# Scan scores as 64 by 64 blocks in the two column halves of TensorE

## The chip, the cores and the metric

The kernel runs on one core of a Trainium2 chip. The metric is the device time of one execution in microseconds (us).

## The reference

Two layers of a network on 1152 tokens (1024 of a latent sample and 128 of a prompt) with 1024 channels. Layer 0 mixes tokens by Fourier transforms, layer 1 by a gated linear recurrence in both directions (HGRN2, 8 heads with 128 key and 128 value channels); each is followed by an MLP of 4096 channels. What the change touches is the recurrence of layer 1. Cut to what matters:

```python
f = lbh + (1.0 - lbh) * jax.nn.sigmoid(z)      # z: forward and backward gate projections
k = 1.0 - f
...
def step(s, inp):                              # one chunk of tokens
    bcum = jnp.cumsum(gc, axis=-2)             # gc = log f
    o_inter = jnp.einsum('dbhtk,dbhkv->dbhtv', qc * jnp.exp(bcum), s)
    decay = jnp.exp(jnp.where(tril[:, :, None], diff, -jnp.inf))
    scores = jnp.einsum('dbhtk,dbhsk,dbhtsk->dbhts', qc, kc, decay)
    o_intra = jnp.einsum('dbhts,dbhsv->dbhtv', scores, vc)
    s_new = jnp.exp(blast[..., 0, :])[..., None] * s + jnp.einsum('dbhsk,dbhsv->dbhkv', ...)
    return s_new, o_inter + o_intra
```

The score of query t and key s is a product over the key channels with the gates between s and t. The size of a chunk is free in exact arithmetic; the kernel takes chunks of 128 tokens.

## The kernel before

Activations lie channel-major: channels on the 128 partitions, 1152 token columns, in three column chunks of 384 for the projections and MLPs and in nine chunks of 128 (`NK`) for the scan. Weights and activations of the large products are split into a high and a low part, and `mm3` (L85) makes each product from three one-pass matmuls, recorded as L91. The scan's own products are plain float32, which TensorE runs as two weight loads and two matmuls each.

`hgrn` (L634) works head by head. `heads_in(h)` computes the two gate projections and the query of a head (three projections of 72 matmuls), `gates(h)` the output gate (72 more), `values(p)` the values of two heads. `levels(F, q)` (L716) makes the scores of all nine chunks, `finish` (L772) the states, the outputs and their norm. In the loop at L845 head h runs `levels` and `finish`, and the projections of head h + 1 are written after them.

In `levels`, `QK` holds queries and keys with the gates multiplied in, for both directions. Scores are built by doubling block sizes B = 1, 2, ... 64 (seven levels). A first call of `scores` (L740) takes the products of queries and summed keys on the diagonal and has ScalarE copy them from PSUM to `sT` (L741). Each level then has four steps:

- ScalarE copies the keys of the level to `V` (L751; one buffer, so the copy waits for the scores of the level before);
- `scores` (L733) multiplies, for each chunk, 128 keys by 128 queries on TensorE (L737), three chunks to a PSUM buffer; queries of the two directions are read in alternating blocks by `view` (L726), at level 0 column by column;
- VectorE copies each group of three chunks to `sT` where the level's mask says so (`copy_predicated`, L753). The mask of a level selects pairs of tokens in the same block of 2B but different halves of it;
- VectorE multiplies keys and queries by the gates of the level (L762) and halves the list of gates (L765).

```python
def scores(lhs, rhs, done):
    for g in range(NK // 3):
        ps = self.t(pp, [P, 4, P], F32, "o", 3)[:, 0:3, :]
        for i in range(3):
            nc.tensor.matmul(out=ps[:, i, :], lhsT=lhs(3 * g + i), rhs=rhs(3 * g + i), start=True, stop=True)
        done(slice(3 * g, 3 * g + 3), ps)
```

`finish` transposes the keys (L779, copied by ScalarE at L781), updates the states (L786, L799, L825) and sums each chunk's output from scores and states (L818 to L821).

The order of the instructions on each engine is not written out by hand. The framework lists them when the kernel is built, by data dependence, by the order in the program and by its estimate of each instruction's time, so that work of the next head stands between the score calls of one head. At run time every engine takes its list in that order. PSUM has three banks with tag "o" (scores, outputs), three with "z" (projections) and two with "m". The small weight matmuls of `ada_pe` (L156: two weight columns, 512 moving columns, and L165: two rows) belong to layer 0 and are named only because the prediction reads them.

Of the kernel before, what the change touches and what calls it, by code (L numbers as in the profile page):

```python
# [19 lines left out]
P = 128  # L20
# [19 lines left out]
def spans(c):  # L40
    """Column ranges of chunk c with the index of their conditioning vector."""
    a, b = c * CH, (c + 1) * CH
    out = []
    if a < LS:
        out.append((a, min(b, LS), 0))
    if b > LS:
        out.append((max(a, LS), b, 1))
    return out
# [7 lines left out]
class Net:  # L56
# [13 lines left out]
    def tmp(self, *shape):  # L70
        """short-lived float32 rows"""
# [4 lines left out]
    def split(self, pool, src, shape, tag, bufs=None):  # L76
        """src == hi + lo, both in the tensor engine's one-pass float32 format."""
# [7 lines left out]
    def mm3(self, out, pairs, first=True, last=True):  # L85
        """out = sum of lhsT^T rhs over pairs of split operands."""
# [30 lines left out]
    def cond_rows(self):  # L117
        """silu of both conditioning vectors on every partition"""
# [17 lines left out]
    def make_A(self, layer, part, g):  # L136
        """norm weight times (1 + scale)"""
# [6 lines left out]
    def bank(self, tag):  # L144
        """one PSUM bank"""
        return self.t(self.ps, [P, 512], F32, tag, {"z": 3, "o": 3, "m": 2}[tag])

    def ada_pe(self, layer, part, tag):
        """one part of silu(cond) @ ada_w on the tensor engine, then channels onto partitions"""
# [20 lines left out]
    def ada_dve(self, layer, part, rawp, junkp, bufs):  # L170
        """the same on the vector engine: rows of the transposed weight times silu(cond), summed along the row"""
# [15 lines left out]
    def fnet(self):  # L187
# [11 lines left out]
        # tokens: position table, rms, and the sums and differences of the two halves  # L199
# [27 lines left out]
        # with a, b, c, d the tokens l, l + 512, 512 - l and 1024 - l (tokens 256 and 768 stand in c and d at l = 0),  # L227
        # even positions take a + b and c + d, cosines of odd ones (a - b) - (c - d) and sines (a - b) + (c - d)
# [61 lines left out]
        # output map, to be folded over the symmetric channel frequencies  # L290
# [104 lines left out]
        def shift():  # L395
            """what the shift adds to position 0: two more columns, one per conditioning vector"""
# [26 lines left out]
        # the residual, channel-major  # L423
# [74 lines left out]
    def square(self, d, chunks):  # L498
        """add the squares of channel tile d to the running sum"""
# [10 lines left out]
    def rstd(self, chunks):  # L510
        """1/rms of the columns of the chunks, columns on partitions"""
# [14 lines left out]
    def rms(self, chunks, tag):  # L526
        """1/rms of the columns of each chunk, on every partition (in PSUM)"""
# [13 lines left out]
    def norm_h(self, c, rb, A, sh):  # L541
        """modulated norm of chunk c, split, channel-major"""
# [15 lines left out]
    def unit(self, src, pool=None, bufs=2):  # L558
        """one split weight unit"""
# [11 lines left out]
    def mlp(self, layer, before_chunk, before_block, after_chunk):  # L571
# [3 lines left out]
        for blk in range(NBLK):  # L575
# [10 lines left out]
            # the first two units go chunk by chunk, as the norm delivers them  # L586
# [47 lines left out]
    def hgrn(self, xd, after_chunk):  # L634
# [52 lines left out]
        def values(p):  # L687
            """values of two heads, tokens on partitions; each goes where its head's output will replace it"""
# [27 lines left out]
        def levels(F, q):  # L716
# [9 lines left out]
            def view(base, B, c=None):  # L726
                np_, off = (T // (2 * B), 0) if c is None else (P // (2 * B), c * P)
# [5 lines left out]
            def scores(lhs, rhs, done):  # L733
                for g in range(NK // 3):
                    ps = self.t(pp, [P, 4, P], F32, "o", 3)[:, 0:3, :]
                    for i in range(3):
                        nc.tensor.matmul(out=ps[:, i, :], lhsT=lhs(3 * g + i), rhs=rhs(3 * g + i), start=True, stop=True)  # L737
                    done(slice(3 * g, 3 * g + 3), ps)

            scores(lambda c: ks[:, 0, c * P:(c + 1) * P], lambda c: q[:, c * P:(c + 1) * P],  # L740
                   lambda sl, ps: nc.scalar.copy(out=sT[:, sl, :], in_=ps))  # L741
# [387 lines left out]
```

## Time and profile before

| | |
|---|---|
| median of 3 runs | 2748.15 us (2743.88 to 2750.95) |
| span of the profiled execution | 2739.4 us (no other time of that execution is given) |
| TensorE busy, matmuls | 2702.2 us, 99% of the span |
| TensorE busy, weight loads | 2582.3 us, 94% |
| VectorE busy | 1453.2 us, 53% |
| ScalarE busy | 854.4 us, 31% |
| GpSimd busy | 35.8 us, 1% |
| the scan with its projections | from about 1121 to 1850 us of the span |

PE stands for TensorE's matmuls, PEld for its weight loads, DVE for VectorE, ACT for ScalarE, POOL for GpSimd. A busy share of 99% on PE means that some matmul was under way; matmuls overlap, so a sum of their records is more than the time they take, and the pace is read from a run of equal ones. The span is the time from the first to the last instruction; what lies around it is the difference to the run's time.

### The profile page before, as it was taken

Reading aid. Unit: us, or ns where it says so; the run is one execution under the profiler, and the core shown is the slowest. Engines: PE = TensorE matmul, PEld = TensorE weight load, DVE = VectorE, ACT = ScalarE, POOL = GpSimd, SP = SyncE. Lnnn points to the kernel's source line nnn. Section 1 sums busy time; section 2 is a strip of 40 time slices with the busy share of each in tenths; the row PEclk is TensorE's granted clock in tenths of the full one; section 3 lists DMA queues with packets and bytes.
Section 4 is the critical chain, followed back from the end, with each engine's and each line's share of the span. In section 5 each row is a group of like instructions: output and inputs, shape, how many; then the busy total and the mean of one; then the engine's idle time right before and its main releaser. Section 6 shows DMA issues by size and latency. Waiting matters only on the chain.

```text
span 2739.4 us, 39068 instructions
## 1 busy us (share of the span) xinstructions
PE 2702.2 (99%) x16142; PEld 2582.3 (94%) x16142; DVE 1453.2 (53%) x2585; ACT 854.4 (31%) x1678; POOL 35.8 (1%) x44
## 2 busy tenths in 40 slices
PE   8999999999999999999999999999999999999999
PEld 3678999999999999999999999999999999999998
DVE  7778998332332447565673774786433233233335
ACT  5435232133123233322332332343422321321332
POOL 0000000000000000000000000000000000000000
PEclk9999999999999999999999999999999999999999
DMA  7531554111111102101000101031111111111111
GB/s 272 200 130 64 184 192 150 43 47 39 40 48 38 62 24 94 35 25 36 28 29 30 36 28 39 28 104 54 43 38 48 43 39 47 43 36 46 45 33 70
DMA packets 65627, 179.93 MB, mean 66 GB/s; under 512 B 8197, under 2 KB 14725, under 8 KB 65449
## 3 DMA queue, kind: packets, MB, share of 16 engines
q1 hardware_dynamic: 65448, 177.43, 19.5%
q8 instruction: 127, 2.08, 0.3%
q14 instruction: 52, 0.42, 0.1%
HBM read 166.92 MB, written 10.49 MB: 65 GB/s over the span
## 4 chain that ended last, share of the span: by engine, by line
PE 91%; DVE 5%; DMA 2%; issue 1%; ACT 1%; POOL 1%; SPq 0%; DVEq 0%; POOLq 0%; ACTq 0%
PE z L91 45%; PE o L91 29%; PE o L737 5%; PE z L702 4%; DMA adaw<-in_ada 2%; DVE junk L179 1%; PE o L156 1%; PE m L786 1%; PE m L779 1%; DVE QK L762 1%; PE m L156 1%; PE o L821 0%; PE o L818 0%; PE o L820 0%; DVE hl L553 0%
## 5 line engine op out<-in xcount | busy, mean ns | idle before, releaser
L91 PE MATMUL z<-hh,wh 128*128 128x384 f32 x2496 | 841.6, 338 | 2.3 <-ACT wh L81 1.3
L91 PE MATMUL z<-hl,wh 128*128 128x384 f32 x2496 | 837.7, 336 | 0.1
L91 PE MATMUL z<-hh,wl 128*128 128x384 f32 x2496 | 836.5, 336 | 0.0
L91 PEld LDWEIGHTS z<-hh,wh 128*128 128x128 f32 x2496 | 468.5, 188 | 7.1 <-ACT hh L552 2.8
L91 PEld LDWEIGHTS z<-hl,wh 128*128 128x128 f32 x2496 | 469.1, 188 | 2.6 <-DVE hl L553 1.5
L91 PEld LDWEIGHTS z<-hh,wl 128*128 128x128 f32 x2496 | 468.6, 188 | 0.6 <-DVE wl L82 0.5
L567 DVE SCALAR_TENSOR_TENSOR x<-o,mod,x 128x384 f32<-128x384 f32 (+2 forms) x512 | 253.2, 515 | 352.0 <-PE o L91 351.6
L82 DVE TENSOR_TENSOR wl<-raw,wh 128x1024 fp32r<-128x1024 f32 x113 | 138.1, 1223 | 293.0 <-ACT wh L81 292.9
L91 PE MATMUL o<-a1h,w 128*128 128x384 f32 x1024 | 280.6, 335 | 0.3 <-DVE x L567 0.3
L91 PE MATMUL o<-a2h,w 128*128 128x384 f32 x1024 | 279.1, 335 | 0.0
L91 PE MATMUL o<-a0h,w 128*128 128x384 f32 x1024 | 279.0, 335 | 0.0
L605 ACT CAST w<-raw 128x512 fp32r<-128x512 f32 x128 | 79.4, 621 | 611.1 <-PE o L91 596.1
L81 ACT CAST wh<-raw 128x1024 fp32r<-128x1024 f32 x113 | 118.5, 1050 | 258.8 <-PE z L91 230.6
L91 PEld LDWEIGHTS o<-a1h,w 128*128 128x128 f32 x1024 | 186.6, 188 | 1.4 <-DVE x L567 0.9
L91 PEld LDWEIGHTS o<-a2h,w 128*128 128x128 f32 x1024 | 186.6, 188 | 0.8 <-issue 0.5
L91 PEld LDWEIGHTS o<-a0h,w 128*128 128x128 f32 x1024 | 186.6, 188 | 0.5 <-ACT a0h L81 0.2
L582 ACT ACTIVATE s<-z 128x384 f32<-128x384 f32 x192 | 93.6, 489 | 284.1 <-PE z L91 277.7
L91 PE MATMUL o<-a2l,w 128*128 128x384 f32 x512 | 171.9, 336 | 0.4 <-DVE a2l L82 0.4
L91 PE MATMUL o<-a0l,w 128*128 128x384 f32 x512 | 171.4, 335 | 0.1
L91 PE MATMUL o<-a1l,w 128*128 128x384 f32 x512 | 171.2, 334 | 0.1
L762 DVE TENSOR_TENSOR QK<-QK,F 128x1152 f32<-128x1152 f32 x112 | 164.2, 1506 | 0.0
L179 DVE SCALAR_TENSOR_TENSOR junk<-adaw,s_rows 128x1024 bf16<-128x1024 f32 x128 | 156.0, 1219 | 11.7 <-DMA adaw<-in_ada 10.6
(256 smaller groups left out, 3281.6 us busy)
## 6 DMA issues: line engine op xcount, KB each, us to landing
adaw<-in_ada SPq DMA_DIRECT2D x96, 512.0 KB, 3.6
raw<-in_w SPq DMA_DIRECT2D x64, 512.0 KB, 3.3
raw<-in_w SPq DMA_DIRECT2D x128, 256.0 KB, 2.6
raw<-in_win SPq DMA_DIRECT2D x32, 512.0 KB, 3.2
x<-in_xT SPq DMA_DIRECT2D x8, 576.0 KB, 4.4
xd<-x SPq DMA_DIRECT2D x8, 576.0 KB, 2.8
raw<-in_who SPq DMA_DIRECT2D x9, 512.0 KB, 3.9
x<-xd SPq DMA_DIRECT2D x8, 576.0 KB, 4.8
```

The source lines that it names most:

```text
L81: nc.scalar.copy(out=hi, in_=src)
L82: nc.vector.tensor_sub(out=lo, in0=src, in1=hi.bitcast(F32))
L91: self.nc.tensor.matmul(out=out, lhsT=w[a], rhs=h[b], start=first and i == 0, stop=last and i == n - 1)
L156: nc.tensor.matmul(out=rows[i][0:2, :], lhsT=self.s[:, k, :], rhs=w[:, i * 512:(i + 1) * 512], start=k == 0, stop=k == KT - 1)
L179: nc.vector.scalar_tensor_tensor(out=jk, in0=w, scalar=1.0, in1=self.sb[:, b, :], op0=ALU.mult, op1=ALU.mult, accum_out=m[:, j, b:b + 1])
L567: self.nc.vector.scalar_tensor_tensor(out=xs, in0=ps[:, a - c * CH:b - c * CH], scalar=gt[:, d, q:q + 1], in1=xs, op0=ALU.mult, op1=ALU.add)
L582: nc.scalar.activation(out=s, in_=z, func=AF.Relu)
L605: nc.scalar.copy(out=w[:, 0], in_=raw)
L702: nc.tensor.matmul(out=half, lhsT=hs[c][a][:, KT // 2 * hf + k, o:o + P], rhs=ws[hf][b][:, k, :], start=hf == 0 and k == 0 and m == 0, sto ...
L737: nc.tensor.matmul(out=ps[:, i, :], lhsT=lhs(3 * g + i), rhs=rhs(3 * g + i), start=True, stop=True)
L762: nc.vector.tensor_tensor(out=kv, in0=kv, in1=fv, op=ALU.mult)
L779: nc.tensor.transpose(out=pt[:, i * P:(i + 1) * P], in_=QK[:, 2 + dr, c * P:(c + 1) * P], identity=self.ident)
```

## The change

The scores of a chunk are computed as blocks of 64 keys by 64 queries instead of 128 by 128. Block h of a chunk (h = 0, 1) is a matmul with 64 weight columns whose output goes to partitions 64h to 64h + 63, the half of the array's columns that belongs to them. The first call and the levels B = 1 to 32 take only the two blocks on the diagonal, the last level (B = 64) only the two off it (`cross`). A call has two PSUM buffers, of five and four chunks, instead of three of three chunks, and four copies of 64 partitions instead of three of 128. At the last level all of a block is wanted, so it is copied by ScalarE without a mask. The rest of the diff takes out comments. The core of it:

```diff
-            def view(base, B, c=None):
-                np_, off = (T // (2 * B), 0) if c is None else (P // (2 * B), c * P)
+            H2 = P // 2
+
+            def view(base, B, c=None, h=0):
+                np_, off = (T // (2 * B), 0) if c is None else (H2 // (2 * B), c * P + h * H2)
...
-            def scores(lhs, rhs, done):
-                for g in range(NK // 3):
-                    ps = self.t(pp, [P, 4, P], F32, "o", 3)[:, 0:3, :]
-                    for i in range(3):
-                        nc.tensor.matmul(out=ps[:, i, :], lhsT=lhs(3 * g + i), rhs=rhs(3 * g + i), start=True, stop=True)
-                    done(slice(3 * g, 3 * g + 3), ps)
-
-            scores(lambda c: ks[:, 0, c * P:(c + 1) * P], lambda c: q[:, c * P:(c + 1) * P],
-                   lambda sl, ps: nc.scalar.copy(out=sT[:, sl, :], in_=ps))
+            def scores(lhs, rhs, done, cross=0):
+                for cs in ((0, 5), (5, 9)):
+                    n = cs[1] - cs[0]
+                    ps = self.t(pp, [P, 512], F32, "o", 3)[:, 0:n * H2].rearrange("p (n t) -> p n t", t=H2)
+                    for i in range(n):
+                        for h in range(2):
+                            nc.tensor.matmul(out=ps[h * H2:(h + 1) * H2, i, :], lhsT=lhs(cs[0] + i, h),
+                                             rhs=rhs(cs[0] + i, h ^ cross), start=True, stop=True)
+                    for h in range(2):
+                        k = h ^ cross
+                        done(sT[h * H2:(h + 1) * H2, cs[0]:cs[1], k * H2:(k + 1) * H2], ps[h * H2:(h + 1) * H2], n, h, k)
+
+            def half(x, c, h):
+                return x[:, c * P + h * H2:c * P + (h + 1) * H2]
+
+            scores(lambda c, h: half(ks[:, 0], c, h), lambda c, h: half(q, c, h),
+                   lambda out, ps, n, h, k: nc.scalar.copy(out=out, in_=ps))
...
-                m = mask[:, lev, :].unsqueeze(1).broadcast_to([P, 3, P])
+                def merge(out, ps, n, h, k):
+                    if 2 * B == P:
+                        nc.scalar.copy(out=out, in_=ps)
+                    else:
+                        m = mask[h * H2:(h + 1) * H2, lev, k * H2:(k + 1) * H2]
+                        nc.vector.copy_predicated(out=out, mask=m.unsqueeze(1).broadcast_to([H2, n, H2]), data=ps)
...
-                scores(lambda c: V[:, c * P:(c + 1) * P], lambda c: view(0, B, c),
-                       lambda sl, ps: nc.vector.copy_predicated(out=sT[:, sl, :], mask=m, data=ps))
+                if 2 * B == P:
+                    scores(lambda c, h: half(V, c, h), lambda c, h: half(QK[:, h], c, h), merge, 1)
+                else:
+                    scores(lambda c, h: half(V, c, h), lambda c, h: view(0, B, c, h), merge)
```

## Rows read from the trace of the kernel before

**Rows 1.** The page: busy time of TensorE, and the chain that ended last

```profile
PE 2702.2 (99%) x16142; PEld 2582.3 (94%) x16142; DVE 1453.2 (53%) x2585; ACT 854.4 (31%) x1678; POOL 35.8 (1%) x44
...
PE 91%; DVE 5%; DMA 2%; issue 1%; ACT 1%; POOL 1%; SPq 0%; DVEq 0%; POOLq 0%; ACTq 0%
PE z L91 45%; PE o L91 29%; PE o L737 5%; PE z L702 4%; DMA adaw<-in_ada 2%; DVE junk L179 1%; PE o L156 1%; PE m L786 1%; PE m L779 1%; DVE QK L762 1%; PE m L156 1%; PE o L821 0%; PE o L818 0%; PE o L820 0%; DVE hl L553 0%
```

**Rows 2.** Busy us (instructions) in the scan's stretch: PE, PEld, DVE, ACT, POOL; then clock, DMA

```profile
1121.00:1850.00 729.00, 716.29 (x4869) 691.38 (x4868) 476.92 (x700) 227.82 (x524) 20.38 (x24) 1.00 0.11 38
```

**Rows 3.** The chain that ended last, levels of the first head: start, us, what

```profile
1136.56 2.09 PE z L91 x12
1138.65 2.18 PE o L737 x18
1140.82 2.11 PE z L91 x12
```

**Rows 4.** Timeline of VectorE, one level of the first head: start, us

```profile
1139.62 1.84 DVE L753 COPY_PREDICATED sT<-mask,o 128x384 f32<-128x384 uint8 x3
1141.36 2.61 DVE L762 TENSOR_TENSOR QK<-QK,F 128x1152 f32<-128x1152 f32 x2
```

**Rows 5.** Timeline, end of a projection and the first two score calls

```profile
1119.11 0.33 PE L91 MATMUL z<-hl,wh 128*128 128x384 f32 x1
1119.11 0.19 PEld L91 LDWEIGHTS z<-hh,wl 128*128 128x128 f32 x1
...
1121.53 2.17 PE L737 MATMUL o<-q,kT 128*128 128x128 f32 x18
1121.56 1.05 ACT L81 CAST wh<-raw 128x1024 fp32r<-128x1024 f32 x1 [3.50 <-PE z L91]
...
1123.54 3.12 PE L737 MATMUL o<-QK,nacc 128*128 128x128 f32 x18
```

**Rows 6.** Who waited for whom, scan: us in total, times, longest

```profile
PEld o L737 <- issue: 18.7, 46, 1.4
```

**Rows 7.** Timeline, two-column matmuls (L156) between full ones of layer 0

```profile
155.96 0.28 PE L91 MATMUL o<-EY1l,vh 128*128 128x256 f32 x1
...
156.08 0.28 PE L91 MATMUL o<-EY1h,vl 128*128 128x256 f32 x1
...
156.28 0.09 PEld L156 LDWEIGHTS m<-adaw,s_silu 128*2 128x2 f32 x2
156.29 3.59 PE L156 MATMUL m<-adaw,s_silu 128*2 128x512 f32 x8
...
159.81 0.19 PEld L91 LDWEIGHTS z<-EY0h,uh 128*128 128x128 f32 x1 [0.86 <-issue]
159.81 0.39 PE L91 MATMUL z<-EY0h,uh 128*128 128x256 f32 x1
```

**Rows 8.** Groups by line in the scan: busy us, mean ns, idle before

```profile
L753 DVE COPY_PREDICATED sT<-mask,o 128x384 f32<-128x384 uint8 x168 | 99.6, 594 | 15.7 <-PE o L737 10.3
...
L781 ACT COPY kT<-m 128x384 f32<-128x384 f32 x48 | 22.2, 480 | 15.9 <-PE m L779 14.0
...
L799 DVE SCALAR_TENSOR_TENSOR Sb<-Sb,F,m 128x128 f32<-128x128 f32 x56 | 19.4, 346 | 12.3 <-PE m L786 7.2
...
L737 PE MATMUL o<-q,kT 128*128 128x128 f32 x144 | 18.0, 275 | 0.0
...
L683 DVE SCALAR_TENSOR_TENSOR gs<-sg,gn,z 128x384 f32<-128x384 f32 x22 | 13.5, 612 | 19.1 <-ACT sg L652 19.1
...
L741 ACT COPY sT<-o 128x384 f32<-128x384 f32 x24 | 10.9, 484 | 2.6 <-PE o L737 2.6
...
L793 ACT COPY Sf<-m 128x128 f32<-128x128 f32 x16 | 3.9, 266 | 4.6 <-PE m L786 4.6
```

**Rows 9.** Other matmuls (L91) between two score calls, last head: stretch, us, PE busy

```profile
1795.40:1797.80 2.40, 2.40 (x15) 2.26 (x13) 1.00 0.00 0
```

**Rows 10.** Timeline of TensorE, two-row matmuls (L165) of layer 0

```profile
47.03 1.05 PE L165 MATMUL o<-ident,traw 2*128 2x2 f32 x8
```

## The prediction

> **What bounds the kernel now.** I read the page's sums first: TensorE is busy for 2702 of 2739 us and holds 91% of the chain that ended last, the scan's score matmuls (L737) 5% of it [rows 1]. The table by stretch shows that this holds in the scan too (1121 to 1850 us): TensorE 716 of 729 us, VectorE 477, ScalarE 228, at a granted clock of 1.00, the higher of its two levels (2.4 GHz) [rows 2]. So in the scan a microsecond of TensorE is a microsecond of time, as long as TensorE finds other work while a level of the scan waits for VectorE.
>
> The chain inside one head's levels [rows 3] shows how that works: 18 score matmuls, 2.18 us, then 12 matmuls of the next head's projections (L91), 2.1 us, in turn, with no gap. VectorE is just as full there: three masked copies (1.84 us) and two products (2.61 us) follow each other without idle time, so that a level takes 4.27 us by VectorE as well [rows 4]. The two engines are in balance in the levels; outside them VectorE has slack and TensorE has none.
>
> **The change, part by part.** *What the scores cost today.* Each 128x128 float32 product is two weight loads and two matmuls, so nine chunks are 18 pairs. In the first call they take (2.17 - 0.275) / 17 = 0.112 us a pair, 2.01 us in all; at level 0, whose queries are read with a large stride, (3.12 - 0.275) / 17 = 0.167, 3.0 us [rows 5] (one record is 0.275 us [rows 8]). Seven calls at 2.01 and one at 3.0 are 17.1 us a head, 137 us for 8 heads, which is the 5% of the chain.
>
> *What they cost after.* A call has 36 pairs, each with half the weight columns and half the moving columns. No row shows two matmuls in different column halves. If the halves work side by side, a chunk needs half the time; with 2 ns more for twice the instructions, 18 x 0.058 = 1.04 us, at level 0 18 x 0.085 = 1.5 us, 8.8 us a head, 70 us in all: 67 us less. If they don't, a pair of half size costs at least half of 0.112 and the gain is 0. If even size doesn't matter, 36 x 0.112 = 4.0 us a call, 128 us more. I take the first: a pair's load starts with the matmul before it and is shorter with fewer columns (0.09 us with 2, 0.19 with 128) [rows 5, 7], so nothing in a half-wide pair needs the other half of the array. The other two ends are rivals below.
>
> The Trainium skill ("TensorEngine Tiling (Array Packing)", Tiling Modes, Key Properties) says that different tiles can load weights and multiply in parallel, and that a change of tiling mode drains the engine. No run here shows the first; by it the sum stands as it is.
>
> *Going in and out of half-wide mode.* The nearest rows are the two-column matmuls of L156 between full ones [rows 7]. Going in: full matmuls start every 0.12 us, the last at 156.08, the narrow one not at 156.20 but at 156.29: 0.09 us. Coming out: eight narrow ones at 0.428 us end their stream at 159.71; the next full one starts at 159.81 and its record is 0.39 instead of 0.28 us, because its weights were no longer loaded under earlier work: 0.21 us. With half-wide weights exposed on the way in (0.05), that is 0.35 us. Today's entry already loses some of it: before the scores TensorE's loads stood still for 18.7 us in 46 cases [rows 6]. I take 0.3 us. The first call and level 0 stand together, so there are 7 visits a head, 56 in all: 17 us. Bounds 0 and 0.5 us: 0 to 28.
>
> *VectorE.* Three masked copies of 128x384 (0.59 us each) become four of 64 partitions with 320, 320, 256 and 256 columns. A column costs (612 - 346) / 256 = 1.04 ns (L683 against L799) [rows 8], so 0.52 and 0.46 us: 1.96 for 1.77 us, 0.19 more at each of six levels, and 1.77 less at the last. A level's pace by VectorE goes from 4.27 to 4.46 us. That is hidden if TensorE has other work: its scores would leave 4.46 - 1.04 - 0.3 = 3.1 us, 18 projection matmuls of 0.173 us instead of 12. A head's projections have 4 x 72 = 288 and the levels use 72, the second projection's weights are split at 1121.56 us, before the levels begin [rows 5], and three PSUM banks with three gate buffers hold six column chunks, 144 matmuls; 6 x 18 = 108 fit. The order on TensorE is fixed when the kernel is built, by an estimate. That it follows the gap shows in the last head, where 15 matmuls stand in a gap instead of 12 [rows 9]. For gaps not exactly filled I add 3 us. If the cover is missing, rival 2 gives the price.
>
> *ScalarE.* The first call's copies become four, and the last level's four come here from VectorE. At (484 - 266) / 256 = 0.85 ns a column (L741 against L793) [rows 8] they take 0.43 and 0.38 us, 1.6 us together: 0.15 more at the start of a head and 1.6 more at its end. ScalarE is busy for 228 of 729 us, but behind the last level's scores it also copies the transposed keys (L781, 0.48 us each [rows 8]), which free the PSUM banks of TensorE's transposes (L779). If these copies are queued first, up to 1.6 us a head come into TensorE's path, 13 us; projections can stand there, and VectorE drops its 1.77 us at the same place. I take 2 us. A score call now takes two PSUM buffers instead of three, DMA issues don't change, and SP and POOL see nothing: no cost.
>
> *The sum.* -67 + 17 + 3 + 2 = -45 us. The page gives no time of the profiled execution other than its span, 2739.4 us; the median of the runs is 8.75 us above it, which I leave as it is. Span 2694, time 2703. Own range of this case: 2683 (no cost of the mode) to 2725 (0.5 us a visit, ScalarE's copies half on the path).
>
> **The rivals.** *1. The halves don't work side by side (slower).* Its place is the weight load. Eight pairs with two moving columns took 1.05 us [rows 10], 0.13 us each with the last one's tail, against 2.17 / 18 = 0.12 for pairs with 128 [rows 5]: the load sets the pace as much as the stream does. If the loads of the two halves follow each other, a half-wide pair can't go below about 0.056 to 0.060 us, a call takes 2.0 to 2.16 us and the mode comes on top: 17 + 64 x (0 to 0.15) + 2 = 19 to 29 us. Time 2771. It decides from 47 ns a pair on, (2.01 - 0.3) / 36: above that the change loses. For it: in the whole trace loads and matmuls alternate, each load starting with the matmul before it [rows 5, 7]; an order this strict would leave the other half waiting. Against it: that is one array with one set of weights in waiting. Chance 0.32.
>
> *1b.* A half-wide load isn't hidden under a matmul at all: a pair then costs its load and its stream, 0.056 + 0.056 = 0.112 us, 128 + 17 us more, 2893. Every row of the full array shows the load hidden. Chance 0.04. The Trainium skill ("TensorE: Matmul & The Clock Gate", Part 3, "What overlaps and what doesn't") has a rule to this effect: a weight load overlaps a running matmul only where the row group differs, and both halves here use all 128 rows. The trace of the full array disagrees.
>
> *2. The order stays as it is.* The scores get shorter, but twelve matmuls still stand in each gap, and TensorE waits for VectorE's 4.46 us. Then five gaps lose 0.19 each, 0.95 us a head; the first call with level 0 still wins 5.0 - 2.55 - 0.3 = 2.1 and the last level 0.7. Together 1.9 us a head, 15 us: 2733. Chance 0.12.
>
> *3. Part of the overlap.* At 45 to 50 ns a pair gain and mode cost cancel: 2740 to 2756, no change. Chance 0.09.
>
> **How the numbers follow.** The forecast has 0.43. Faster by over 0.3% (8 us, about what a measurement of this kernel can tell from no change): the forecast and rival 2, 0.55. Slower: rivals 1 and 1b, 0.36. Within: rival 3, 0.09. The signs are nearly even, because the one number that decides, the pace of half-wide pairs in turn, is in no row. The range therefore reaches from the forecast's best end to the far end of rival 1, 2683 to 2778; outside it lie 1b and what I have not thought of.
>
> **What would show it.** Right: the 36 score matmuls of a call in about 1.05 us with starts some 29 ns apart on average, gaps with about 18 projection matmuls, L737 at 2 to 3% of the chain, the scan near 685 us. Mode cost: 0.1 us of standstill before the first score and a longer first projection behind the last. Rival 1: starts 56 ns apart or more and the scan longer than 729 us. 1b: 112 ns. Rival 2: TensorE idle for VectorE (L762) in every gap, a level at 4.46 us. The forecast's sign is wrong if the starts are over 47 ns apart.

## The result and the profile after

The changed kernel takes 2717.13 us (median of 4 runs, 2716.04 to 2719.05), the kernel before 2747.97 us in the same series (2743.88 to 2750.95): ratio 0.9894, 95% interval 0.9880 to 0.9908, or 30.8 us less, where 45 us less was forecast. The kernel is faster, by the mechanism of the forecast, and a third of the expected gain is missing.

The page of the changed kernel, its sums and its chain that ended last:

```profile
PE 2659.8 (98%) x17294; PEld 2528.4 (93%) x17294; DVE 1457.8 (54%) x2609; ACT 865.6 (32%) x1718; POOL 35.7 (1%) x44
...
PE 84%; DVE 10%; DMA 3%; issue 2%; ACT 1%; POOL 1%; SPq 0%; DVEq 0%; POOLq 0%; ACTq 0%
PE z L91 42%; PE o L91 30%; PE z L702 4%; DVE QK L783 4%; DVE sT L764 3%; DMA adaw<-in_ada 2%; PE o L156 1%; PE m L807 1%; PE o L744 1%; DVE junk L179 1%; PE m L800 1%; PE o L839 1%; PE m L156 1%; DVE wl L82 0%; PE o L842 0%
```

Against [rows 1] the scores (now L744) fall from 5% to 1% of the chain. VectorE rises from 5% to 10%, with the products (L783) and the masked copies (L764) of the levels: work that was beside TensorE's now stands on the path.

The groups by line, the changed operations (busy us, mean ns of one, then idle time ahead and its releaser):

```profile
L744 PE MATMUL o<-QK,nacc 128*64 128x64 f32 x2016 | 78.6, 233 | 24.6 <-DVE QK L783 23.7
...
L764 DVE COPY_PREDICATED sT<-mask,o 64x320 f32<-64x320 uint8 x96 | 50.1, 522 | 3.4 <-PE o L744 0.7
...
L764 DVE COPY_PREDICATED sT<-mask,o 64x256 f32<-64x256 uint8 x96 | 43.0, 447 | 3.1
...
L744 PE MATMUL o<-q,kT 128*64 128x64 f32 x288 | 11.4, 226 | 0.0
```

The same group of the kernel before (its first calls stand in [rows 8]):

```profile
L737 PE MATMUL o<-QK,nacc 128*128 128x128 f32 x1008 | 133.9, 288 | 8.5 <-DVE QK L762 8.4
```

Twice as many score matmuls are busy for 90 us instead of some 152, but TensorE waits 23.7 us ahead of them for VectorE's products, where it waited 8.4. One level of VectorE in the second head, from its timeline (start, us):

```profile
1212.40 2.03 DVE L764 COPY_PREDICATED sT<-mask,o 64x320 f32<-64x320 uint8 x4
1214.46 2.63 DVE L783 TENSOR_TENSOR QK<-QK,F 128x1152 f32<-128x1152 f32 x2
1217.12 2.04 DVE L764 COPY_PREDICATED sT<-mask,o 64x320 f32<-64x320 uint8 x4
```

From copy to copy it is 4.72 us: 2.06 for the copies and 2.66 for the products. In [rows 4] it was 4.27, with the products 1.74 us behind the copies.

Where the time went shows in two stretches: from the first score of the first head to the first score of the last one, and from there to the next norm. The table by stretch of the kernel before (busy time of each engine, granted clock, DMA share, GB/s):

```profile
1125.00:1784.00 659.00, 648.74 (x4406) 627.45 (x4405) 419.51 (x608) 198.73 (x457) 17.83 (x21) 1.00 0.09 31
1784.00:1873.00 89.00, 86.55 (x570) 82.93 (x568) 68.50 (x109) 33.87 (x73) 2.55 (x3) 1.00 0.32 110
```

and of the changed kernel:

```profile
1125.00:1751.00 626.00, 611.14 (x5446) 578.33 (x5444) 424.20 (x632) 210.41 (x497) 17.83 (x21) 1.00 0.10 33
1751.00:1847.00 96.00, 82.45 (x707) 78.51 (x706) 69.75 (x111) 35.68 (x78) 2.55 (x3) 0.91 0.30 102
```

By the starts of the first score calls, seven heads take 625.4 us instead of 662.7 (37.3 less), but the last head up to the next norm takes 96.3 instead of 88.5 (7.7 more); TensorE is idle there for 13.5 of 96 us, at a granted clock of 0.91, where it was idle for 2.5 of 89 at 1.00. Together 29.6 us less, against 30.8 by the medians. All that follows takes 866.6 us in both. What stands ahead of the scan has the same code and ends between 1121.5 and 1129.8 us in the profiles of this study; its 4.3 us more in this profile are that spread.

The levels themselves did not get shorter. From the start of a head's first score call to the start of its last one it is 29.8 to 30.3 us in seven heads of the kernel before and 30.5 to 31.2 in the changed one: VectorE sets their pace. What got shorter is what stands behind them, since 102 to 106 matmuls of the next head's projections lie in a head's gaps instead of 72. At the 0.173 us from one to the next, 30 to 34 matmuls are 5.2 to 5.9 us (an estimate); each of the seven heads gains 5.1 to 5.5 us.

The last head's scores in TensorE's timeline of the changed kernel (start, us, count, idle time ahead):

```profile
1758.86 1.30 PE L744 MATMUL o<-QK,nacc 128*64 128x64 f32 x36 [0.82 <-DVE QK L783]
...
1763.51 1.27 PE L744 MATMUL o<-QK,nacc 128*64 128x64 f32 x36 [0.16 <-DVE QK L783]
...
1765.52 0.34 PE L91 MATMUL z<-hh,wh 128*128 128x384 f32 x1
1768.22 1.27 PE L744 MATMUL o<-QK,nacc 128*64 128x64 f32 x36 [2.37 <-DVE QK L783]
1772.91 2.19 PE L744 MATMUL o<-QK,nacc 128*64 128x64 f32 x36 [3.42 <-DVE QK L783]
1777.82 2.19 PE L744 MATMUL o<-QK,nacc 128*64 128x64 f32 x36 [2.72 <-DVE QK L783]
1782.73 2.19 PE L744 MATMUL o<-QK,nacc 128*64 128x64 f32 x36 [2.73 <-DVE QK L783]
```

Eighteen filling matmuls (L91) stand ahead of the first of these calls, seventeen ahead of the second, five ahead of the third, and from 1765.9 us on none: four calls alone in 17 us. In [rows 9] and the calls around it there were 15, 15, 15, 12, 12 and 11. From 1771 to 1785 us the table by stretch has a granted clock of 0.50, the lower level (1.2 GHz); ahead of that TensorE stood idle for 2.37 and for 3.42 us with a single call between:

```profile
1771.00:1785.00 14.00, 6.64 (x109) 6.24 (x110) 13.21 (x17) 3.34 (x7) 0.00 (x0) 0.50 0.00 1
```

A call then takes 2.19 us instead of 1.27, but it follows the one before it after 4.91 us instead of 4.71: with VectorE setting the pace, the lower clock costs about 0.2 us in each of three levels there, a small part of what the last head loses.

### The profile page after: what moved, and what is told of

It is laid out like the page before. It is cut to its first block, busy times and chain, and to the rows that moved or that the text cites. A ratio compares the mean times of both kernels' runs of the same rounds, so it can differ in the third digit from the quotient of the medians.

```text
span 2714.1 us, 41391 instructions
## 1 busy us (share of the span) xinstructions
PE 2659.8 (98%) x17294; PEld 2528.4 (93%) x17294; DVE 1457.8 (54%) x2609; ACT 865.6 (32%) x1718; POOL 35.7 (1%) x44
## 4 chain that ended last, share of the span: by engine, by line
PE 84%; DVE 10%; DMA 3%; issue 2%; ACT 1%; POOL 1%; SPq 0%; DVEq 0%; POOLq 0%; ACTq 0%
PE z L91 42%; PE o L91 30%; PE z L702 4%; DVE QK L783 4%; DVE sT L764 3%; DMA adaw<-in_ada 2%; PE o L156 1%; PE m L807 1%; PE o L744 1%; DVE junk L179 1%; PE m L800 1%; PE o L839 1%; PE m L156 1%; DVE wl L82 0%; PE o L842 0%
## 5 line engine op out<-in xcount | busy, mean ns | idle before, releaser
L91 PE MATMUL z<-hh,wh 128*128 128x384 f32 x2496 | 840.0, 338 | 1.6 <-ACT wh L81 0.6
L91 PE MATMUL z<-hl,wh 128*128 128x384 f32 x2496 | 840.7, 337 | 0.1
L91 PE MATMUL z<-hh,wl 128*128 128x384 f32 x2496 | 837.1, 336 | 0.0
L91 PEld LDWEIGHTS z<-hh,wh 128*128 128x128 f32 x2496 | 468.3, 188 | 7.3 <-ACT hh L552 2.7
L91 PEld LDWEIGHTS z<-hl,wh 128*128 128x128 f32 x2496 | 469.0, 188 | 4.5 <-DVE hl L553 1.4
L91 PEld LDWEIGHTS z<-hh,wl 128*128 128x128 f32 x2496 | 468.8, 188 | 0.9 <-DVE wl L82 0.2
L567 DVE SCALAR_TENSOR_TENSOR x<-o,mod,x 128x384 f32<-128x384 f32 (+2 forms) x512 | 253.2, 515 | 352.1 <-PE o L91 351.7
L91 PE MATMUL o<-a1h,w 128*128 128x384 f32 x1024 | 280.7, 335 | 0.0
L91 PE MATMUL o<-a2h,w 128*128 128x384 f32 x1024 | 279.2, 335 | 0.0
L91 PE MATMUL o<-a0h,w 128*128 128x384 f32 x1024 | 279.1, 335 | 0.0
L82 DVE TENSOR_TENSOR wl<-raw,wh 128x1024 fp32r<-128x1024 f32 x113 | 138.3, 1224 | 261.9 <-ACT wh L81 261.1
L91 PEld LDWEIGHTS o<-a1h,w 128*128 128x128 f32 x1024 | 186.7, 188 | 0.8 <-DVE x L567 0.3
L91 PEld LDWEIGHTS o<-a2h,w 128*128 128x128 f32 x1024 | 186.6, 188 | 0.8 <-PE o L91 0.3
L91 PEld LDWEIGHTS o<-a0h,w 128*128 128x128 f32 x1024 | 186.6, 188 | 0.4 <-ACT a0h L81 0.2
L91 PE MATMUL o<-a2l,w 128*128 128x384 f32 x512 | 172.0, 336 | 2.9 <-DVE a2l L82 2.9
L91 PE MATMUL o<-a0l,w 128*128 128x384 f32 x512 | 171.4, 335 | 0.1
L91 PE MATMUL o<-a1l,w 128*128 128x384 f32 x512 | 171.4, 335 | 0.2 <-DVE a1l L82 0.2
L783 DVE TENSOR_TENSOR QK<-QK,F 128x1152 f32<-128x1152 f32 x112 | 165.0, 1513 | 1.5
L179 DVE SCALAR_TENSOR_TENSOR junk<-adaw,s_rows 128x1024 bf16<-128x1024 f32 x128 | 156.1, 1220 | 12.9 <-DMA adaw<-in_ada 11.7
```

The source lines that it names most:

```text
L82: nc.vector.tensor_sub(out=lo, in0=src, in1=hi.bitcast(F32))
L91: self.nc.tensor.matmul(out=out, lhsT=w[a], rhs=h[b], start=first and i == 0, stop=last and i == n - 1)
L179: nc.vector.scalar_tensor_tensor(out=jk, in0=w, scalar=1.0, in1=self.sb[:, b, :], op0=ALU.mult, op1=ALU.mult, accum_out=m[:, j, b:b + 1])
L567: self.nc.vector.scalar_tensor_tensor(out=xs, in0=ps[:, a - c * CH:b - c * CH], scalar=gt[:, d, q:q + 1], in1=xs, op0=ALU.mult, op1=ALU.add)
L783: nc.vector.tensor_tensor(out=kv, in0=kv, in1=fv, op=ALU.mult)
```

## The experiments

All start from the changed kernel. Each series has runs of the kernel before on its own chip, so the ratios are what compares. "Seven heads" and "last head" are the two stretches above, read from each kernel's profile, in us.

| kernel | time, us | before, us | ratio, 95% interval | seven heads | last head |
|---|---|---|---|---|---|
| before | 2747.97 | | 1 | 662.7 | 88.5 |
| changed | 2717.13 | 2747.97 | 0.9894 (0.9880 to 0.9908) | 625.4 | 96.3 |
| e1_halves_in_turn | 2735.56 | 2742.86 | 0.9975 (0.9965 to 0.9984) | 643.3 | 98.3 |
| e2_last_level_masked | 2712.26 | 2742.86 | 0.9889 (0.9876 to 0.9903) | 623.1 | 96.3 |
| e3_copies_over_128 | 2694.31 | 2742.86 | 0.9818 (0.9805 to 0.9832) | 613.7 | 89.4 |
| e4_last_head_filled | 2710.19 | 2742.86 | 0.9883 (0.9870 to 0.9897) | 625.1 | 91.6 |
| after_again | 2712.75 | 2744.62 | 0.9884 (0.9867 to 0.9900) | 625.2 | 97.0 |
| e5_last_head_on_vector | 2716.09 | 2744.62 | 0.9897 (0.9882 to 0.9912) | 625.1 | 95.6 |
| e6_level5_by_scalar_filled | 2715.24 | 2744.62 | 0.9896 (0.9881 to 0.9911) | 630.2 | 92.4 |
| e7_level5_by_scalar | 2717.87 | 2744.62 | 0.9905 (0.9891 to 0.9920) | 630.2 | 94.0 |
| after_third | 2714.59 | 2745.09 | 0.9892 (0.9877 to 0.9907) | 625.2 | 95.5 |
| e8_masked_and_filled | 2710.18 | 2745.09 | 0.9872 (0.9857 to 0.9887) | 623.5 | 93.0 |
| e9_filled_with_less_gpsimd | 2712.47 | 2745.09 | 0.9879 (0.9863 to 0.9896) | 623.2 | 93.3 |

The changed kernel's seven heads repeat within 0.2 us and its last head within 1.5 us. Many of the effects below are smaller than the intervals of the whole time; they are told by these stretches, each read from one execution. The times expected below start from the first series, where the kernel before takes 2747.97 us; in the later ones it takes 3 to 5 us less.

**Do the two halves work side by side?**

```diff
-                    for i in range(n):
-                        for h in range(2):
+                    for h in range(2):
+                        for i in range(n):
```

> All 4 or 5 blocks of the upper half of the columns are computed before those of the lower half, so that neighbouring score matmuls go to the same half; nothing else is changed. Theory (the gain comes from two halves that work side by side): with the neighbours in one half a block takes the 56 to 60 ns that half a pair took before the change, a call takes 2.0 to 2.2 us instead of 1.05 us, and 64 calls give back 1.0 us each less what falls into TensorE's waits for VectorE (some 8 to 12 us): 2765 to 2785 us. Rival (a block of half the size is cheap by itself, whichever half its neighbour is in): starts stay 30 ns apart and the time stays at 2713 to 2721 us.

One call in TensorE's timeline, first of the changed kernel, then of this one:

```profile
1142.56 1.27 PE L744 MATMUL o<-QK,nacc 128*64 128x64 f32 x36 [0.30 <-DVE QK L783]
1143.76 0.44 PE L91 MATMUL z<-hh,wh 128*128 128x384 f32 x1
1144.04 0.34 PE L91 MATMUL z<-hl,wh 128*128 128x384 f32 x1
```

```profile
1219.13 1.77 PE L744 MATMUL o<-QK,nacc 128*64 128x64 f32 x36
```

In the changed kernel's levels the single records start some 22 and 36 ns apart in turn, 58 ns for a block in each half; from the first start to the last a call takes 1.047 us. With the halves in turn, neighbours in one half start 53 to 60 ns apart, a call takes 1.553 us, and the two stretches take 20 us longer (by the ratios the time rises by 0.8 to 0.9% of before, 22 to 25 us). So the halves do work side by side, and a block of half the size isn't cheap by itself: the rival falls. The size was missed, +0.5 us a call where +1.0 was expected. Where a group of blocks in one half gives way to the other half's, records start within 3 to 6 ns of each other: the other half's first blocks start beside the last ones of the half before, nine of 36 in most calls. Order by halves costs half of the overlap, not all of it.

**What is the unmasked copy worth by itself?**

```diff
-                    if 2 * B == P:
-                        nc.scalar.copy(out=out, in_=ps)
-                    else:
+                    if True:
```

> The last level is copied with the mask by VectorE again; the blocks of 64 by 64 stay. The four copies put about 2.1 us back on VectorE once in each head and take four copies from ScalarE. Theory (VectorE's levels are what the order waits for in the changed kernel): up to 2.1 us in each of 8 heads come back, 2725 to 2734 us. Rival (the last level lies beside filling matmuls and ScalarE's copies cost the same wait): 2713 to 2721 us, and the unmasked copy is worth nothing by itself.

The rival holds, and more: seven heads take 2.3 us less with the mask. ScalarE's timeline behind the last level of one head shows why, first of the changed kernel:

```profile
1339.80 1.62 ACT L761 COPY sT<-o 64x320 f32<-64x320 f32 x4 [3.01 <-PE o L744]
1341.44 0.86 ACT L802 COPY kT<-m 128x384 f32<-128x384 f32 x2
```

and of this kernel, where the second line is the first:

```profile
1336.38 0.86 ACT L800 COPY kT<-m 128x384 f32<-128x384 f32 x2 [3.96 <-PE m L798]
```

The four unmasked copies hold ScalarE for 1.62 us ahead of the copies of the transposed keys, which free the banks of TensorE's transposes; on VectorE they cost this stretch nothing. The part "without a mask" costs 0.3 us a head, and the blocks carry the whole gain.

**What do copies of 64 partitions cost?**

```diff
-                    for h in range(2):
-                        k = h ^ cross
-                        done(sT[h * H2:(h + 1) * H2, cs[0]:cs[1], k * H2:(k + 1) * H2], ps[h * H2:(h + 1) * H2], n, h, k)
+                    done(sT[:, cs[0]:cs[1], cross * H2:(cross + 1) * H2], ps, n)
```

> The blocks of both halves are copied by one instruction over 128 partitions, two copies in a level instead of four, into columns 0:64 (last level 64:128) of the score tile. This changes a part of the computation: the blocks stand in other columns than the reference's, and the lower partitions of the masked levels copy other elements; TensorE's work and the elements for each partition are the same. Theory (the copies of 64 partitions make VectorE's level 4.73 us, and TensorE waits about 0.3 us for it in three or four gaps of a head): VectorE's level falls to 3.6 to 3.9 us, TensorE's idle time ahead of the score line (24.6 us) falls below 8 us, and the time to 2695 to 2707 us. Rival (the level is set by TensorE, the waits only move): 2712 to 2720 us. The last head, where filling matmuls are missing, should still show score calls that follow each other with nothing between.

VectorE's timeline (start, us) and the groups by line of this kernel:

```profile
1314.76 0.83 DVE L762 COPY_PREDICATED sT<-mask,o 128x320 f32<-128x320 uint8 x2
1315.49 2.59 DVE L781 TENSOR_TENSOR QK<-QK,F 128x1152 f32<-128x1152 f32 x2
1318.35 0.92 DVE L762 COPY_PREDICATED sT<-mask,o 128x320 f32<-128x320 uint8 x2 [0.27 <-PE o L744]
```

```profile
L744 PE MATMUL o<-QK,nacc 128*64 128x64 f32 x2016 | 76.9, 232 | 10.6 <-DVE QK L781 10.6
...
L762 DVE COPY_PREDICATED sT<-mask,o 128x320 f32<-128x320 uint8 x48 | 24.7, 515 | 5.2 <-PE o L744 4.2
```

A copy takes the same time for 64 and for 128 partitions (522 and 515 ns with 320 columns), so half as many take half the time, and they follow each other faster too: the products start 0.73 us behind the first of two copies, where two of 64 partitions need 2.06 / 2 = 1.03. A level takes 3.6 us, VectorE now waits 0.27 us for TensorE, and the waits ahead of the scores fall from 24.6 to 10.6 us (below 8 was expected). Ratio 0.9818: some 19 us under the changed kernel, 11.7 of them in seven heads and 7 in the last one. The theory holds: VectorE's copies are what the order waits for. The last head still has its last three calls with nothing between (fills of 13, 12, 13 and 2, 40 in all as in the changed kernel), and yet takes 89.4 us: from its first score call to its last it is 24.3 us instead of 31.5, and what stands behind takes 65.1 instead of 64.7. Faster copies don't bring the missing filling back; they gain about as much in another place.

**Can the last head be filled?** Its filling matmuls are the first tiles of the output projection, 42 for each chunk of columns. They need the heads' outputs in two parts, a rounded one by ScalarE and the rest by a subtraction (L885) on VectorE, and of the 21 subtractions for the first seven heads the last seven stood behind the levels.

```diff
+                if between:
+                    between(lev)
...
-            nc.vector.tensor_sub(out=oh[c][1][:, h, :], in0=oTs[h][:, cs], in1=oh[c][0][:, h, :].bitcast(F32))
+            e = nc.gpsimd if c and h < HEADS - 1 else nc.vector
+            e.tensor_tensor(out=oh[c][1][:, h, :], in0=oTs[h][:, cs], in1=oh[c][0][:, h, :].bitcast(F32), op=ALU.subtract)
...
+        todo = [[lambda: wo(ws[0], 0, 0, [(k, k) for k in range(HEADS - 1)]), lambda: [take(h, 1) for h in range(2, HEADS - 1)]],
+                [lambda: wo(ws[1], 1, 0, [(k, k) for k in range(HEADS - 1)])],
...
+        st = levels(F, q, between)
```

> Only the last head's order is changed: the output projection's early tiles (42 matmuls for each column chunk) are written between the levels, 21 a gap, and the subtractions for the low parts of chunks 1 and 2 are done by GpSimd. Theory (the last head loses about 13 us since its filling matmuls wait for low parts that stand behind VectorE's levels): every gap of the last head is filled, the clock of that stretch stays at 0.98 or more, and most of the idle time there comes back: 2704 to 2711 us. Rival 1 (VectorE's own chain sets the end of the last head, the filling matmuls only move): 2714 to 2720 us. Rival 2 (GpSimd's subtractions come later than the gaps, TensorE waits for them in its fixed order): over 2720 us.

VectorE's timeline in the last head's first levels, and GpSimd's:

```profile
1754.15 2.07 DVE L764 COPY_PREDICATED sT<-mask,o 64x320 f32<-64x320 uint8 x4
1756.25 4.33 DVE L785 TENSOR_TENSOR QK<-QK,F 128x1152 f32<-128x1152 f32 x2
1760.61 0.62 DVE L567 SCALAR_TENSOR_TENSOR x<-z,mod,x 128x384 f32<-128x384 f32 x1
1761.14 2.04 DVE L764 COPY_PREDICATED sT<-mask,o 64x320 f32<-64x320 uint8 x4
1763.21 3.48 DVE L785 TENSOR_TENSOR QK<-QK,F 128x1152 f32<-128x1152 f32 x2
...
1769.31 2.63 DVE L785 TENSOR_TENSOR QK<-QK,F 128x1152 f32<-128x1152 f32 x2
```

```profile
1746.00 19.46 POOL L884 TENSOR_TENSOR hl<-x,hh 128x384 fp32r<-128x384 f32 x14 [21.51 <-ACT hh L882]
```

All six gaps hold 20 or 21 matmuls, the granted clock of its levels (1750 to 1788 us) is 1.00, and the last head takes 91.6 us instead of 96.3: about 5 of the 13 us that the expectation names. The whole time (ratio 0.9883) can't be told from the changed kernel's. The levels themselves got longer (36.9 us from the start of the first score call to the start of the last, 31.5 before the edit), for two reasons that these rows show: the residual additions of the filling tiles (L567, 0.62 us each) stand on VectorE in the levels, and the products are slower while GpSimd subtracts. What stands behind the levels takes 54.7 us instead of 64.7. Part of the idle time was a lack of filling; part of it is VectorE's own work, which filling brings forward and doesn't remove.

**Is it GpSimd that slows the products?** Two kernels: the same order with all subtractions on VectorE (`e = nc.vector`), and, with later runs, e9. The changed kernel was run again beside it.

> The changed kernel once more, unaltered, beside the other three of this call, as their yardstick. Expected: the stretches head by head repeat (182.4 us for two heads, 96.3 us from the last head's first score to the next norm), 2711 to 2719 us.

> The last head's filling matmuls are written between the levels as in e4_last_head_filled, but all subtractions for the low parts stay on VectorE. In e4 the products of the last head's first two levels took 4.33 and 3.48 us where 2.64 us is usual, in the stretch where GpSimd subtracted (14 at 1.43 us). Theory (GpSimd at work slows VectorE): the products take 2.6 to 2.8 us again, the ten subtractions of chunks 1 and 2 add 0.55 us each to VectorE in the levels, and the stretch from the last head's first score to the next norm stays within 2 us of e4's 91.6 us: the same price by another way. Rival (those products were late for another reason, such as the order of the matmuls): products stay near 3.5 to 4.3 us and the stretch grows past 94 us.

The expectation had a mistake: a head's first level always has slow products, 3.69 us in the changed kernel and not 2.64. Against that GpSimd's share in e4 is 4.33 - 3.69 = 0.64 and 3.48 - 2.64 = 0.84 us. In e5, without GpSimd, the second level's two products take 1.36 and 1.35 us (2.7 together):

```profile
1761.12 1.36 DVE L785 TENSOR_TENSOR QK<-QK,F 128x1152 f32<-128x1152 f32 x1
1762.51 0.62 DVE L567 SCALAR_TENSOR_TENSOR x<-z,mod,x 128x384 f32<-128x384 f32 x1
1763.05 0.55 DVE L884 TENSOR_TENSOR hl<-x,hh 128x384 fp32r<-128x384 f32 x1
```

So GpSimd was the cause: e6 and e8, where GpSimd does the same work as in e4, have the same slow products, and e9, where it ends before them, has none. One product and one subtraction of e4, from the timelines of VectorE and GpSimd, show how:

```profile
1756.25 3.14 DVE L785 TENSOR_TENSOR QK<-QK,F 128x1152 f32<-128x1152 f32 x1
```

```profile
1757.03 4.42 POOL L884 TENSOR_TENSOR hl<-x,hh 128x384 fp32r<-128x384 f32 x1
```

A first product takes 2.49 us without GpSimd, and a subtraction by GpSimd 1.0 us when it meets no such operation of VectorE. Here the product, begun beside an earlier subtraction that ends at 1757.1, takes 0.65 us more, and the next subtraction lasts until 0.9 us after VectorE's second product, which itself takes its usual 1.34 us. The two engines seem to take turns, an instruction at a time; that is read from these times and not tested further. In all VectorE loses some 2.5 us in e4's last head: 1.5 in the products, the rest in two subtractions of its own (L82 with 1.46 us instead of 1.22, L884 with 1.36 instead of 0.55).

But e5's stretch takes 95.6 us: with the subtractions on VectorE nearly all of e4's gain is lost again, against "within 2 us of e4". In these two orders GpSimd is the better place in spite of what VectorE loses. How much of the 4 us between them is VectorE's subtractions isn't shown, since the order moved too: e5's gaps hold 28, 21, 37, 21, 17 and 0 matmuls.

**Fewer masked copies by VectorE.** Level 5, whose entries are whole rectangles of 32 by 32, copied by ScalarE without a mask:

```diff
+                    if B == 32:
+                        for r in range(2):
+                            a, b = r * 32, 32 - r * 32
+                            nc.scalar.copy(out=out[a:a + 32, :, b:b + 32], in_=ps[a:a + 32, :, b:b + 32])
```

> e2's masked last level and level 5 by ScalarE's rectangles, with the last head's order as in the changed kernel. Theory: two heads take 180.5 to 182 us (182.4 in the changed kernel, 181.9 in e2), the last head's levels 1 to 2 us less: 2706 to 2712 us. Rival (ScalarE becomes late): two heads take over 182.4 us, 2713 us or more.

> Three edits together: e4's last head, e2's masked last level, and level 5 (blocks of 32), whose masked copies are replaced by eight ScalarE copies of rectangles of 32 partitions by 32 columns, which are exactly that level's entries. VectorE loses 2.06 us a head. Theory (VectorE's copies are what lengthens the levels): level 5's wait goes (about 0.3 us a head), the last head's levels lose up to 2 us, together with e4 and e2 some 3 to 10 us under the changed kernel of this call: 2703 to 2711 us. Rival (ScalarE, with eight more copies, delays the copies of V or the PSUM buffers): 2711 to 2722 us.

The rival holds in both: seven heads take 630.2 us, 7 more than e2. ScalarE's timeline in one head of e7:

```profile
1333.58 2.24 ACT L763 COPY sT<-o 32x160 f32<-32x160 f32 x8 [1.69 <-PE o L744]
1335.85 1.25 ACT L772 COPY nacc<-QK 128x576 f32<-128x576 f32 x2
```

and the first matmuls of the next level's call in TensorE's:

```profile
1336.57 0.45 PE L744 MATMUL o<-QK,nacc 128*64 128x64 f32 x4 [0.60 <-ACT nacc L772]
```

Eight small copies take 2.24 us, as long as VectorE's four, and ScalarE's copies for the next level's scores (L772) stand behind them: TensorE waits 0.60 us for them. Its order also splits the next level's call, 4 scores, 2 filling matmuls, 32 scores, one more change of mode. The last head gains 2 us by it (94.0); for the others it is a loss.

**Put together.** e2 and e4 in one kernel, and the same with GpSimd for chunk 1 only and chunk 2 behind the levels:

> The changed kernel, unaltered, as the yardstick of this call: 2711 to 2719 us.

> e2's masked last level (0.27 us a head shorter in its trace) and e4's last head (91.6 us from the last head's first score to the next norm, where the changed kernel has 96.3 to 97.0) in one kernel. If the two add up: 7 times 0.27 us and some 5 us, 6 to 8 us under the yardstick of this call, 2704 to 2710 us. Rival (the last head's VectorE, with the masked copies again, gives up e4's gain): within 3 us of the yardstick.

> As e8_masked_and_filled, but GpSimd subtracts for chunk 1 only (7 instead of 14) and the matmuls of chunk 2 with their subtractions, on VectorE, come after the levels: four gaps of the last head are filled, the last two are not. Theory (in e4 GpSimd's 19.5 us of work beside VectorE stretched the products of the first two levels, 4.33 and 3.48 us against 3.69 and 2.64 us in the changed kernel, and with every gap filled nothing is left to lie beside the state updates that follow): the second level's products fall to 2.6 to 2.9 us and the stretch from the last head's first score to the next norm to 88 to 91 us. Rival (the work put off comes back on VectorE behind the levels): 92 us or more.

Apart from e3, which changes a part of the computation, e8 is the fastest kernel of this study: 2710.18 us (2708.41 to 2710.88) beside 2714.59 (2713.25 to 2718.89) for the changed kernel, 4.4 us less, where 6 to 8 were expected if the two add up and at most 3 by the rival; the intervals of the two ratios still overlap. In e9 the second level's products fall to 1.36 and 1.35 us, as expected, but the last head takes 93.3 us, not 88 to 91: the work put off comes back behind the levels. The theory was right on the products and wrong on the time.

## Why the prediction was right, and where it was wrong

For seven heads its sum can be checked term by term; predicted terms are scaled by 7/8.

- **The scores, right.** Predicted 36 pairs in 1.04 us a call; measured 1.047. Added up over all calls of seven heads, from the first start to the last, 117.1 us became 62.0: 55 less, predicted 59.
- **The mode, right in place, too dear.** The second matmul behind the last score starts 0.434 us after it, before the change 0.290 (medians): 0.144 us, seen above in the record of 0.44 us. On the way in, the gap from the last L91 to the first score is 0.268 us in e3, where it is seldom lengthened by a wait, against 0.249 before: 0.02. So 0.16 us a visit instead of 0.3, about 9 us instead of 15, at 56 visits in seven heads where 49 were counted: the order splits one more call in each head. L156 was a fair model of the way out; on the way in today's kernel already paid nearly all of it, of which the prediction took off too little.
- **The order follows the gap, right for seven heads.** 15 to 19 matmuls, mostly 17 or 18, stand in a gap instead of 12. Rival 2 is out.
- **VectorE hidden, wrong.** Predicted 4.46 us a level, measured 4.72. The single copies were sized well (0.52 and 0.45 us); that they would follow each other as before was not: copies to products is 2.06 instead of 1.74, products to copies 2.66 instead of 2.52. And 18 matmuls did not cover it: time ahead of the scores beyond the change of mode went from 8.6 to 15.6 us, 7 more where "gaps not exactly filled" had 2.6.
- **ScalarE, right in size.** Predicted 1.75 for seven heads, 2.3 by e2, which puts the masked copies back. Against the kernel before, TensorE's transposes and outputs behind the levels take only 0.7 us more.

-55 + 9 + 7 + 2 = -37 us, measured -37.3, predicted -39.4. Read from TensorE's intervals alone it is -55 + 10 + 7 + 0.7. That the sum comes so near is in part luck: the scores gained 4 us less than predicted and the cover cost 4 more, while the mode cost 5 or 6 less.

Two more points of the recorded working. Its own upper end, 2725 us, follows with all 13 us of ScalarE's copies on the path; with the half that it names the terms give 2719. And the whole range, 2683 to 2778 us, lies on both sides of the kernel before, so that the measured time falls into it says little. What speaks for the mechanism is the pace of the pairs.

**The step that failed** is the cover of the last head. The prediction took from [rows 9] that the order follows the gap, counted the projections of a next head, 6 x 18 of 144 matmuls, and multiplied by eight heads. The last head has no next one. Its 15 matmuls of [rows 9] came from the output projection, which needs VectorE: subtractions for its low parts ahead of a tile, a residual addition (L567) behind it. In the kernel before, VectorE takes one of each between the masked copies of the levels, here the subtraction:

```profile
1795.17 0.54 DVE L864 TENSOR_TENSOR hl<-x,hh 128x384 fp32r<-128x384 f32 x1
```

In the changed kernel the next ones come only behind the last score call, the residual addition at 1789.80 us:

```profile
1786.24 1.49 DVE L885 TENSOR_TENSOR hl<-x,hh 128x384 fp32r<-128x384 f32 x3
```

The filling ended after 40 matmuls, where the kernel before has 80 and the prediction had counted 108, and the last head went from 88.5 to 96.3 us: 7.7 lost instead of 5.6 gained, 13.3 of the 14 us by which the forecast of the change (-45 against -31) was off. Split at the start of its last score call, the head takes 31.5 instead of 31.0 us ahead and 64.7 instead of 57.6 behind. The 40 matmuls put off are 6.9 us at 0.173 us each, and the 68 that the count has too many 11.8 of the 13.3 us (estimates). So the last head lost by missing filling and hardly by the pace of its levels. Filling these gaps costs something itself: in e4 the stretch behind gets 10 us shorter and the levels 5.4 longer, since this filling, unlike a next head's projections, brings VectorE's work along. Why the framework's order put VectorE's operations behind the levels isn't shown; in e5, where the program has them between the levels, VectorE does them there.

Rival 1, with its price of 19 to 29 us more than before, is out by the starts, and even e1, whose order comes nearest to it, stays 7 us under before. The Trainium skill ("TensorE: Matmul & The Clock Gate", Part 3, "What overlaps and what doesn't") has a weight load overlap a running matmul only in other row groups. This case's trace disagrees: both halves use all 128 rows, and 36 loads and matmuls start within 1.047 us. That tiles work independently, as the Trainium skill ("TensorEngine Tiling (Array Packing)", Key Properties) has it, is what the runs show. That section of the Trainium skill also says that a change of mode drains the engine; the runs show 0.16 us a visit, without telling a drain from the weight load that is no longer hidden.

## What to carry to other kernels

Where another engine sets the pace, shorter work doesn't shorten the stretch; it makes room, and the gain is what moves into the room. So ask for each place what fills the gap next, and on which engine that filling depends: the last turn of a loop often has another filling than the others. Splitting a block over the array's halves also splits what reads it, and a masked copy costs by its columns, not by its partitions (522 ns for 64, 515 for 128); count the readers' instructions before the matmuls'. In an order written for two halves, alternate between them.

## What the runs showed that was not expected

- Two masked copies of 64 partitions reach the next instruction after 1.03 us, two of 128 partitions with the same columns after 0.73 (changed kernel and e3). Why the small ones don't run into each other isn't shown.
- Blocks put in order by halves still overlap where the half changes: 1.553 us a call, between 1.047 (in turn) and the 2.0 that 35 steps of 58 ns would take.
- GpSimd at work beside VectorE lengthens products of two tensors in SBUF (3.69 to 4.33 and 2.64 to 3.48 us), and such a product holds up GpSimd as well (a subtraction of 4.42 us where 1.0 is usual), while the masked copies, whose data come from PSUM, keep their 2.04 to 2.07 us (e4). The Trainium skill ("GPSIMD Engine Reference", 1. Specifications) names contention with VectorE instructions of two SBUF inputs; the trace agrees.
- With TensorE idle between the last head's score calls, the granted clock fell to 0.50 (1771 to 1785 us), and a call went from 1.27 to 2.19 us; with the gaps filled (e4) the clock of the last head's levels stayed at 1.00.
